# Down projection of a hybrid encoder layer as seven block products, decays from exponents of sums, the first norm scaled ahead of its transposes, and a refitted instruction order

## The chip, the cores and the metric

The kernel runs on one core of one Trainium2 chip. The metric is the time of one launch on the device in microseconds, as the median of several runs. TensorE multiplies, VectorE (DVE), ScalarE (ACT) and GpSimd (POOL) do the elementwise work, and loads and stores are issued by SyncE (SP) or by ScalarE. Products are written to PSUM, eight banks of 128 x 512 float32.

## The reference

One layer, 512 tokens, width 1024, all in float32. Cut to what matters:

```python
h = rmsnorm(x, mix_norm[l])                       # 512 x 1024
p = h @ w_in[l]                                   # 1024 x 9248
rx, ry, qkv, z, ba, gates = jnp.split(p, SPLIT_IDX, axis=-1)
y_rnn = rglru_branch(rx, ry, ...) @ w_rnn_proj[l] # conv, gates, a scan forwards and one backwards
y_dn = deltanet_branch(qkv, z, ba, ...) @ w_dn_proj[l]
x = x + (g_rnn * y_rnn + g_dn * y_dn) @ w_out[l]
h = rmsnorm(x, ffn_norm[l])
gt, up = jnp.split(h @ w_gate_up[l], 2, axis=-1)  # 2 x 2816
x = x + (jax.nn.silu(gt) * up) @ w_down[l]        # 2816 x 1024
return rmsnorm(x, final_norm)

# inside deltanet_branch, for 8 heads and both directions:
gc = jnp.cumsum(g, axis=-1)
decay = jnp.exp(jnp.where(incl, gc[..., :, None] - gc[..., None, :], -jnp.inf))
A = jnp.where(strict, jnp.einsum("nhcid,nhcjd->nhcij", kb, k) * decay, 0.0)
att = jnp.einsum("nhcid,nhcjd->nhcij", q, k) * decay
```

## The kernel before, in words

Activations lie with features on the 128 partitions and the 512 tokens along the free dimension, so a weight block of 128 x 128 is the stationary operand and 512 tokens stream. Each float32 operand is split into a high part (`whi`, `hh`, `fh`), a rounded copy that ScalarE makes, and a low part (`wlo`, `hl`, `fl`), the rest, that VectorE subtracts. A product is three matmuls: high x high, high x low and low x high. Weights come from DRAM into one of three raw tiles (`wraw`) by a load on SP's queue; the split goes into one of two pairs of tiles `whi`, `wlo`, or into tiles of the pools `t2` (14 tiles of 128 x 512) and `t4` (22 tiles of 128 x 1024). In the profile both pools read `t`.

The stages follow one another: first norm; input projection with the recurrent branch (12 blocks in groups of three) and the first heads' convolutions; four pairs of delta-net heads (`dn_front`, `dn_mats`, `dn_inverse`, `dn_state`, `dn_out`), between which the rest of the input projection and the gates run; output projection; second norm; gate and up projection; down projection; last norm.

**First norm.** `norm_scale` makes a diagonal `dg` of a token's reciprocal norm (VectorE), and `norm_transpose` multiplies the token rows by it on TensorE, which transposes and scales at once, in full float32. ScalarE then writes the high part times the gain, VectorE the low part.

**Decays.** In `dn_mats` each head and direction needs exp(gc_i - gc_j) for four chunks of 128 tokens. VectorE multiplies a triangular mask with the high and the low part of the gate column `gh`, `gl` (two 512-wide products), TensorE multiplies them with the triangular `slr` or `sur` (two 512-wide matmuls), which gives the differences of the sums, ScalarE takes the Exp of all 512 columns, and GpSimd zeroes what lies outside the triangle.

**Gate and up.** From the third k-tile of 22 on, `gate_up` already uses a seven-product form of a 2 x 2 block product (256-column matmuls): the blocks are the two halves of the contraction, gate and up, and the two halves of the tokens.

**Down projection.** For each half of the 1024 output columns `down_mm` goes through eleven pairs of k-tiles, four token chunks and three products; tokens are the stationary operand, 512 weight columns stream. The last chunk's second half is done in two pieces of 256 columns. The last three k-pairs of the second half are held so that each chunk ends by itself and its final norm (`down_end`, a root, a reciprocal, two scalings and the stores) runs while the next chunk multiplies.

**The order.** Every instruction is recorded first with a cost and a due time, and `Plan.order` then simulates the engines: the instruction with the earliest due time whose inputs are ready and whose tiles are free goes next. The due times of the stages are a table of numbers, `TIMES`; costs are formulas in `Rec.__getattr__`, times a factor `SLACK`. Where a wait between two engines is counted, `LAG` has it. Each engine then gets its instructions in that order, and so does SP's queue of loads. `spend` opens a new stage. All instructions are issued from one line of `Rec`, so the profile shows L374 throughout, and groups are told apart by their tiles.

Of the kernel before, what the change touches and what calls it, by code (L numbers as in the profile page):

```python
# [32 lines left out]
RELEASE = 200  # L33
SLACK = {"ACT": 1.1, "DVE": 1.1, "POOL": 1.2}
LOOK = 40
TIMES = [
# [18 lines left out]
class Plan:  # L55

# [5 lines left out]
    LAG = {("PE", "PE"): 0, ("PE", "DVE"): 250, ("PE", "ACT"): 250, ("DVE", "PE"): 320, ("ACT", "PE"): 320, ("POOL", "PE"): 320,  # L62
           ("DVE", "DVE"): 130, ("DVE", "ACT"): 250, ("ACT", "ACT"): 50, ("ACT", "DVE"): 200, ("DVE", "POOL"): 250,
           ("POOL", "DVE"): 150, ("ACT", "POOL"): 250, ("SP", "SP"): 0}

    def __init__(self, nc):
        self.nc = nc
        self.ops = []
        self.where, self.bases = [], []
        self.t = self.base = 0.0  # L70
# [7 lines left out]
        self.fixed = 13.3  # L78
# [40 lines left out]
    def add(self, eng, fn, outs, ins, cost, tail=0.0, table=None):  # L119
# [22 lines left out]
        cost *= SLACK.get(eng, 1.0)  # L142
        self.ops.append((eng, fn, deps, touched, round(cost), round(1.25 * tail), table, self.t))
# [3 lines left out]
    def order(self):  # L147
# [13 lines left out]
        for i, o in enumerate(ops):  # L161
            for d in o[2]:
                users[d].append(i)
        uses, first, last = {}, {}, {}
# [7 lines left out]
        need = [sorted((x for x in o[3] if x in self.tile_tag), key=first.get) for o in ops]  # L172
        free = dict(self.tags)
        queue = {tag: [] for tag in self.tags}
        for name, key in first.items():
            queue[self.tile_tag[name]].append((key, name))
# [9 lines left out]
        pe_end, cold = 0, WARM  # L186
        result, start = [], {}

        def slots(i):
            want = [x for x in need[i] if x not in held]  # L190
            taken = {}
            for name in want:
# [8 lines left out]
                for key, other in queue[tag]:  # L201
# [38 lines left out]
        while True:  # L240
            for e in ENGINES:
# [7 lines left out]
                for name in want:  # L249
# [4 lines left out]
                    queue[tag].remove((first[name], name))  # L254
                c = o[4]
                if e == "ACT" and o[6] is not None and table not in o[6]:
                    table = o[6][0]
                    c += 1283
                if e == "PE":
                    if now - pe_end > 3000:  # L260
                        cold = 0
                    if cold < WARM:
                        c *= 2
                        cold += c
                    pe_end = now + c
                end = done = now + c
# [18 lines left out]
            while events and events[0][0] == now:  # L285
                _, kind, i = heapq.heappop(events)
                o = ops[i]
                if kind == 0:
                    busy[o[0]] = False
                elif kind == 1:  # L290
# [4 lines left out]
                    for u in users[i]:  # L295
                        left[u] -= 1
                        if not left[u]:
                            wait = 0 if o[5] else self.LAG.get((o[0], ops[u][0]), 200)
# [1153 lines left out]
```

## Time and profile before

| | |
|---|---|
| median of 3 runs | 1097.39 us (1097.16 to 1097.98) |
| profiled execution, first to last instruction | 1095.2 us |
| TensorE matmuls, busy | 1070.3 us, 6916 records |
| VectorE, busy | 826.6 us, 1489 |
| ScalarE, busy | 626.6 us, 1127, of it 60 table loads 77.0 us |
| GpSimd, busy | 46.1 us, 93 |
| read from and written to DRAM | 95.17 MB and 2.10 MB |

A float32 matmul of 128 columns leaves two records, a transpose one. The stages by the trace: the first norm ends near 25 us, the recurrent groups near 250, the heads near 700, the output projection and second norm near 760, gate and up near 960, the down projection at 1089; the store of the last result ends the span. In the rows of the profile "out<-in" names the tiles without their numbers, the figure after the bar is the busy time of the group in us and the mean of one instruction in ns, and what follows is the idle time of the engine just before them with what ended it.

### The profile page before, as it was taken

What the parts mean: (1) busy time and instruction counts of PE and PEld (TensorE: products, weight loads), DVE (VectorE), ACT (ScalarE), POOL (GpSimd) and SP (SyncE); (2) the same over time, 40 slices, a digit from 0 to 9 for tenths busy, and PEclk for the clock granted to TensorE, in tenths of its full rate; (3) what the DMA queues carried; (4) which work ended last, traced back from release to release, by engine and by line L of the source; (5) the groups of instructions that cost most, each with busy time, mean ns of one, the idle gap of its engine ahead of it and who ended that gap; (6) DMA issues with size and microseconds to landing.
All of it is one profiled execution on the core that took longest, in us unless ns stands there. A gap on an engine that the chain in (4) does not pass through costs nothing.

```text
span 1095.2 us, 17616 instructions
## 1 busy us (share of the span) xinstructions
PE 1070.3 (98%) x6916; PEld 933.7 (85%) x6916; DVE 826.6 (75%) x1489; ACT 626.6 (57%) x1127; POOL 46.1 (4%) x93
## 2 busy tenths in 40 slices
PE   7999899999999999999999999999999999999997
PEld 6988678888887878788798888789999999988886
DVE  6686999669994798589759847868898988872432
ACT  6779997797346653766575254446544444451223
POOL 2000000002020010020000000000000000000000
PEclk9999999999999999999999999999999999999999
DMA  7342313232322033104211313441233334332332
GB/s 196 103 116 67 88 55 104 82 92 72 101 82 67 8 111 103 53 20 113 80 35 45 96 49 121 135 140 58 78 116 108 98 104 116 102 111 96 97 97 77
DMA packets 160787, 98.40 MB, mean 90 GB/s; under 512 B 4800, under 2 KB 151344, under 8 KB 160704
## 3 DMA queue, kind: packets, MB, share of 16 engines
q1 hardware_dynamic: 159232, 93.99, 29.6%
q10 hardware_dynamic: 1184, 3.15, 0.8%
q8 instruction: 54, 0.88, 0.3%
q14 instruction: 29, 0.24, 0.1%
q0 software_dynamic: 288, 0.13, 0.0%
HBM read 95.17 MB, written 2.10 MB: 89 GB/s over the span
## 4 chain that ended last, share of the span: by engine, by line
PE 87%; DVE 7%; ACT 4%; issue 1%; DMA 1%; SPq 0%; DVEq 0%
PE mm L374 50%; PE ax L374 22%; PE st L374 15%; DVE t L374 5%; ACT t L374 2%; DVE wlo L374 1%; ACT na L374 1%; DMA wraw<-in_w_in_dram 1%; DVE na L374 1%; ACT whi L374 1%; ACT L374 0%; DVE hl L374 0%; ACT ax L374 0%; SPq L374 0%; ACT hh L374 0%
## 5 line engine op out<-in xcount | busy, mean ns | idle before, releaser
L374 ACT CAST whi<-wraw 128x1024 fp32r<-128x1024 f32 (+2 forms) x150 | 146.6, 978 | 206.8 <-PE mm L374 83.2
L374 DVE TENSOR_TENSOR wlo<-wraw,whi 128x1024 fp32r<-128x1024 f32 (+2 forms) x149 | 168.8, 1135 | 122.3 <-ACT whi L374 75.0
L374 PE MATMUL mm<-hh,whi 128*128 128x512 f32 (+2 forms) x704 | 242.4, 356 | 3.7 <-ACT whi L374 3.6
L374 PE MATMUL mm<-hl,whi 128*128 128x512 f32 (+2 forms) x704 | 241.9, 356 | 0.0
L374 DVE TENSOR_TENSOR t<-t,t 128x512 fp32r<-128x512 f32 (+16 forms) x414 | 212.4, 524 | 17.0 <-ACT t L374 10.4
L374 PE MATMUL mm<-hh,wlo 128*128 128x512 f32 (+1 forms) x688 | 155.6, 356 | 0.0
L374 PEld LDWEIGHTS mm<-hh,whi 128*128 128x128 f32 (+1 forms) x704 | 133.0, 189 | 22.2 <-ACT whi L374 5.0
L374 PEld LDWEIGHTS mm<-hl,whi 128*128 128x128 f32 (+1 forms) x704 | 133.0, 189 | 16.9
L374 PEld LDWEIGHTS mm<-hh,wlo 128*128 128x128 f32 x688 | 115.9, 189 | 16.9
L374 DVE SCALAR_TENSOR_TENSOR t<-mm,par,t 128x511 f32<-128x511 f32 (+1 forms) x108 | 80.0, 743 | 21.0 <-ACT t L374 20.3
L374 PE MATMUL ax<-t,t 32*32 32x32 f32 (+3 forms) x876 | 90.9, 263 | 1.8 <-issue 0.8
L374 PE MATMUL mm<-t,whi 128*128 128x512 f32 x320 | 83.0, 397 | 0.6 <-DVE t L374 0.4
L374 ACT CAST t<-t 128x512 fp32r<-128x512 f32 (+1 forms) x95 | 64.7, 687 | 32.3 <-DVE t L374 29.0
L374 PEld LDWEIGHTS ax<-t,t 128*128 128x128 f32 (+1 forms) x876 | 74.2, 153 | 10.3 <-ACT t L374 2.9
L374 ACT ACT_TABLE_LOAD x60 | 77.0, 1283 | 6.4 <-PEq L1438 1.7
L374 PEld LDWEIGHTS mm<-t,whi 128*128 128x128 f32 x320 | 59.0, 188 | 14.5 <-ACT whi L374 1.9
L374 PE MATMUL mm<-t,t 128*128 128x256 f32 (+1 forms) x372 | 66.4, 322 | 0.0
L374 PEld LDWEIGHTS mm<-t,t 128*128 128x128 f32 x372 | 54.8, 191 | 4.9
L374 ACT ACTIVATE t<-t 128x128 f32<-128x128 f32 (+4 forms) x84 | 45.8, 558 | 13.0 <-DVE t L374 9.5
L374 PE MATMUL mm<-t,wlo 128*128 128x512 f32 x160 | 43.0, 393 | 0.5 <-DVE wlo L374 0.5
L374 PE MATMUL st<-hh,whi 128*128 128x512 f32 (+1 forms) x112 | 42.1, 380 | 0.3 <-ACT whi L374 0.3
L374 PE MATMUL st<-hl,whi 128*128 128x512 f32 (+1 forms) x112 | 41.7, 377 | 0.0
(219 smaller groups left out, 1808.0 us busy)
## 6 DMA issues: line engine op xcount, KB each, us to landing
wraw<-in_w_in_dram SPq DMA_DIRECT2D x72, 512.0 KB, 3.8
wraw<-in_w_gate_up_dram SPq DMA_DIRECT2D x44, 512.0 KB, 3.9
wraw<-in_w_down_dram SPq DMA_DIRECT2D x22, 512.0 KB, 3.7
wraw<-in_w_rnn_proj_dram SPq DMA_DIRECT2D x16, 384.0 KB, 3.6
wraw<-in_w_out_dram SPq DMA_DIRECT2D x8, 512.0 KB, 4.7
wraw<-in_w_dn_proj_dram SPq DMA_DIRECT2D x8, 384.0 KB, 3.5
t<-in_x_dram SPq DMA_DIRECT2D x4, 512.0 KB, 5.3
na<-in_x_dram ACTq DMA_DIRECT2D x4, 512.0 KB, 7.5
```

Source lines behind the costliest of these rows:

```text
L374: self.plan.add(e, lambda: real(*a, **kw), outs, ins, cost, tail, table)
```

## The change

Five things are changed at once.

1. The down projection is done in seven products of half-size blocks and not eight. The 2 x 2 blocks are even and odd k-tiles, the two halves of the output columns (512 each), and the two halves of the tokens (256 each). Products 1, 7, 5 and 6 go first through all eleven k-pairs, into all eight PSUM banks; then the partial sums are combined (`m_`, `v_`) into the residual, and products 2, 4 and 3 add on. `first_x` and `second_x` make the sums of activations and their splits; `down_w` loads and splits the weights of one product for two k-pairs at once.
2. The four sums of weight blocks that the products need are made earlier, by `down_sums`, while the heads run: two loads of 512 KB, four additions on VectorE, two stores of 512 KB to a scratch tensor `dsum` in DRAM for each k-pair. The down projection loads them from there.
3. The decays are no longer multiplied on TensorE. The sums of the gates, one row for each head and direction, are written to a scratch tensor `gsum` once; each head and direction loads its row broadcast to all partitions, GpSimd fills what lies outside the triangle with -1e30, and ScalarE takes four Exps of 128 columns, each with the negative sum (`ngc`) as its bias.
4. The first norm scales the token rows first (half on VectorE, half on ScalarE), and TensorE then only transposes them.
5. The planner's costs are refitted (separate occupancy and latency, longer scans and transposes, a cost for turning TensorE between tile modes, shorter waits between engines, no `SLACK`), and `TIMES` has new values, and more of them, since each step of the down projection is now a stage.

```diff
-RELEASE = 200
-SLACK = {"ACT": 1.1, "DVE": 1.1, "POOL": 1.2}
+RELEASE = 60
+TURN = 115
...
-                elif op in ("tensor_tensor", "tensor_tensor_scan"):
-                    cost = 69 + 1.042 * n
...
-                elif op == "transpose":
-                    cost = 68 + 1.042 * n
+                elif op == "tensor_tensor_scan":
+                    occ = 66 + 2.083 * n
+                elif op == "transpose":
+                    occ = 66 + (1.042 if n <= 256 else 1.99) * n
...
     def norm_scale(src, c):
-        dg = small([P, P], "dg", 4)
-        V.tensor_scalar(dg, ident, rms_rstd(src, c), None, ALU.mult)
-        return dg
+        rin = rms_rstd(src, c)
+        sc = four(shape=(P, D))
+        V.tensor_scalar(sc[:, 0:512], src[:, 0:512], rin, None, ALU.mult)
+        A.activation(sc[:, 512:D], src[:, 512:D], AF.Copy, scale=rin)
+        return sc
...
-                    T.matmul(pt[:, (2 * j + i) * P:(2 * j + i + 1) * P], srcs[i][:, kt * P:(kt + 1) * P], dgs[i], start=True, stop=True)
+                    turn(pt[:, (2 * j + i) * P:(2 * j + i + 1) * P], srcs[i][:, kt * P:(kt + 1) * P])
...
-                rh, rl = two(F32R), two(F32R)
-                mk = (upi if d == 0 else loi).unsqueeze(1).to_broadcast([P, NT, P])
-                for r_, g_ in ((rh, gh), (rl, gl)):
-                    V.tensor_tensor(r_.rearrange("p (c i) -> p c i", c=NT), mk, f(g_[:, c0:c0 + 4]).unsqueeze(2).to_broadcast([P, NT, P]), ALU.mult)
-                pd = axb()
-                lt = slr if d == 0 else sur
-                T.matmul(pd, lt, rh, start=True, stop=False)
-                T.matmul(pd, lt, rl, start=False, stop=True)
                 dt_ = two()
-                act(dt_, pd, AF.Exp)
                 dv = dt_.rearrange("p (c i) -> p c i", c=NT)
-                G.affine_select(out=dv, in_=dv, pattern=[[0, NT], [1 - 2 * d, P]], compare_op=ALU.is_ge, fill=0.0, base=0,
+                Q.dma_start(dt_, grow[d, S * h:S * (h + 1)].partition_broadcast(P))
+                G.affine_select(out=dv, in_=dv, pattern=[[0, NT], [1 - 2 * d, P]], compare_op=ALU.is_ge, fill=-1e30, base=0,
                                 channel_multiplier=2 * d - 1)
+                for c in range(NT):
+                    act(dv[:, c, :], dv[:, c, :], AF.Exp, bias=ngc[:, c0 + c:c0 + c + 1])
...
+    def down_sums(j):
+        spend()
+        now = plan.t
+        re, ro = four(shape=(P, D)), four(shape=(P, D))
...
+        Q.dma_start(re, wdn[:, 2 * j, :])
+        Q.dma_start(ro, wdn[:, 2 * j + 1, :])
...
+        V.tensor_tensor(b11, b11, b12, ALU.add)
+        V.tensor_tensor(b12, b12, b22, ALU.add)
+        V.tensor_tensor(b22, b11, b22, ALU.add)
+        V.tensor_tensor(b21, b22, b21, ALU.add)
+        Q.dma_start(dsum[j, :, 0:2, :], re.rearrange("p (a n) -> p a n", a=2))
+        Q.dma_start(dsum[j, :, 2:4, :], ro.rearrange("p (a n) -> p a n", a=2))
...
+    def first_x(j):
...
+        A.copy(xh[:, 3, :], tt[:, 0, :])
+        V.tensor_tensor(xl[:, 3, :], tt[:, 0, :], f(xh[:, 3, :]), ALU.subtract)
+        V.tensor_tensor(q[:, 0:2, :], tt[:, 0:2, :], tt[:, 1:4:2, :], ALU.subtract)
+        V.tensor_tensor(q[:, 2, :], tt[:, 0, :], q[:, 1, :], ALU.subtract)
+        V.tensor_tensor(tt[:, 1, :], tt[:, 2, :], q[:, 2, :], ALU.subtract)
+        A.copy(xh[:, 0:3, :], q[:, 0:3, :])
+        V.tensor_tensor(xl[:, 0:3, :], q[:, 0:3, :], f(xh[:, 0:3, :]), ALU.subtract)
...
+    banks = {"a": [axb(), axb()], "b": [mmb(), mmb()], "c": [stb(), stb()], "d": [axb(), mmb()]}
+    bank_of = {"1": "a", "6": "b", "7": "c", "5": "d", "2": "a", "4": "c", "3": "d"}
...
+    def down_mm(name, j, i, w, cs=(0, 1), n0=0, n=512):
+        (hi, lo), (xh, xl) = w, xp[name, j]
...
+        for c in cs:
+            po = banks[bank_of[name]][c][:, n0:n0 + n]
+            sh, sl_ = xh[:, c * P:(c + 1) * P], xl[:, c * P:(c + 1) * P]
+            T.matmul(po, sh, hi[:, i, n0:n0 + n], start=begin, stop=False, skip_group_check=sk)
+            T.matmul(po, sh, lo[:, i, n0:n0 + n], start=False, stop=False, skip_group_check=sk)
+            T.matmul(po, sl_, hi[:, i, n0:n0 + n], start=False, stop=end, skip_group_check=sk)
+
+    units = [(j, min(2, NP_ - j)) for j in range(0, NP_, 2)]
+    for j0, n in units:
+        for i in range(n):
+            first_x(j0 + i)
+        for name in ("1", "7", "5", "6"):
+            w = down_w(name, j0, n)
+            for i in range(n):
+                down_mm(name, j0 + i, i, w)
```

Three places of the order. First SP's queue where the first heads' matrices and the recurrent branch's projection are loaded (`wraw` is a weight block, `t` under `in_w_down` a raw k-tile for the sums, `gsum` and `dsum` the two scratch tensors). Before:

```order
L374 DMA wraw_396<-in_w_rnn_proj_dram 128x6x128
L374 DMA wraw_786<-in_w_in_dram 128x8x128
L374 DMA wraw_641<-in_w_in_dram 128x8x128
L374 DMA wraw_773<-in_w_in_dram 128x8x128
L374 DMA wraw_633<-in_w_in_dram 128x8x128
```

And with the change:

```order
L405 DMA t_554<-in_w_down_dram 128x1024
L405 DMA t_555<-in_w_down_dram 128x1024
L405 DMA t_689<-gsum 128x512
L405 DMA t_551<-in_w_down_dram 128x1024
L405 DMA wraw_770<-in_w_in_dram 128x8x128
L405 DMA t_550<-in_w_down_dram 128x1024
L405 DMA t_690<-gsum 128x512
L405 DMA dsum<-t_554 128x1024
L405 DMA wraw_490<-in_w_in_dram 128x8x128
L405 DMA wraw_639<-in_w_in_dram 128x8x128
L405 DMA dsum<-t_550 128x1024
```

Raw k-tiles, broadcast rows and stores of sums now stand between the weight blocks, and a store stands ahead of the next weight block's load.

Second ScalarE at the end of the recurrent branch (`rgs` marks its decay Exp, the 128x1024 forms its square roots, `st` a Gelu, `ngc` the new decays of the heads), with the change:

```order
L405 ACTIVATE t_685<-t_685,ngc_157 128x128
L405 ACT_TABLE_LOAD
L405 ACTIVATE t_494<-t_494 128x1024
L405 CAST whi_401<-wraw_400 128x768
L405 ACTIVATE t_495<-t_495 128x1024
L405 ACTIVATE t_496<-t_496 128x1024
L405 ACT_TABLE_LOAD
L405 ACTIVATE t_685<-t_685,ngc_157 128x128
L405 CAST whi_417<-wraw_416 128x768
L405 ACT_TABLE_LOAD
L405 ACTIVATE t_512<-st_513 128x512
```

Before, one Exp of 512 columns stood for the four pieces of `t_685`; now its pieces stand singly between table loads. Third TensorE in the down projection (`ax`, `st` and `mm` are PSUM banks). Before:

```order
L374 MATMUL ax_1709<-whi_1719,t_1721 128x512
L374 MATMUL ax_1709<-wlo_1720,t_1721 128x512
L374 MATMUL ax_1709<-whi_1719,t_1722 128x512
L374 MATMUL ax_1709<-whi_1719,t_1721 128x512
L374 MATMUL ax_1709<-wlo_1720,t_1721 128x512
L374 MATMUL ax_1709<-whi_1719,t_1722 128x512
```

And with the change:

```order
L405 MATMUL st_1692<-whi_1724,t_1719 128x512
L405 MATMUL ax_1688<-whi_1739,t_1733 128x512
L405 MATMUL ax_1689<-whi_1739,t_1733 128x512
L405 MATMUL st_1693<-whi_1724,t_1715 128x512
L405 MATMUL st_1693<-wlo_1725,t_1715 128x512
L405 MATMUL st_1693<-whi_1724,t_1716 128x512
L405 MATMUL st_1693<-whi_1724,t_1718 128x512
L405 MATMUL st_1693<-wlo_1725,t_1718 128x512
```

A split weight pair now serves 12 matmuls and not 24, and matmuls with the high part of the next pair (`whi_1739`) are drawn ahead of the last ones with this pair.

More of the change, by code (lines that the diff above doesn't have):

```diff
@@ L163, in order @@
                 users[d].append(i)
+        number = {name: i for i, name in enumerate(self.tile_tag)}
         uses, first, last = {}, {}, {}
@@ L200, in slots @@
                 moves, ups = [], 0
-                for key, other in queue[tag]:
+                for key, _, other in queue[tag]:
                     if other == name:
@@ L265, in order @@
                     pe_end = now + c
-                end = done = now + c
+                end, done = now + c, now + l
                 if o[5]:
@@ L289, in order @@
                     busy[o[0]] = False
+                    if o[0] == "PE":
+                        for u in users[i]:
+                            if ops[u][0] == "PE":
+                                left[u] -= 1
+                                if not left[u]:
+                                    insort(ready["PE"], (when[u], u))
                 elif kind == 1:
@@ L516, in trunk @@
     for c0 in (0, 2):
-        norm_transpose(xs[c0:c0 + 2], [norm_scale(xs[c0 + i], i) for i in range(2)], gain, hh, hl, c0)
-        plan.t = -15.0
-    plan.t = 0.0
+        xs = []
+        for c in (c0, c0 + 1):
+            xc = four(shape=(P, D))
+            Q.dma_start(xc, x[0, c * P:(c + 1) * P, :])
+            xs.append(xc)
+        if c0 == 0:
+            gain = load_gain(mix_norm[0], "gain1")
+        norm_transpose([norm_scale(xs[i], i) for i in range(2)], gain, hh, hl, c0)
+        spend()
     prow = two(shape=(P, 2, P))
@@ L1109, in trunk @@
     for g in range(4):
+        for j in range(3 * g, min(3 * g + 3, NP_)):
+            down_sums(j)
         spend()
@@ new lines, in raw_part, with down_w @@
+    def raw_part(par, half):
+        return lambda j, n: wdn[:, 2 * j + par:2 * j + par + 2 * n - 1:2, 512 * half:512 * (half + 1)]
+    wsrc = {"1": raw_part(0, 0), "2": raw_part(1, 0), "3": raw_part(1, 1), "4": sum_part(2), "5": sum_part(0), "6": sum_part(3), "7": sum_part(1)}
+    def down_w(name, j, n, held=False):
+        now = plan.t
+        raw = new(wp, (P, 2, 512), "wraw", 3)
+        if held:
+            hi, lo = four(F32R), four(F32R)
+        else:
+            hi, lo = new(wp, (P, 2, 512), "whi", 2, F32R), new(wp, (P, 2, 512), "wlo", 2, F32R)
+        plan.t = now - 40
+        Q.dma_start(raw[:, 0:n, :], wsrc[name](j, n))
+        plan.t = now - AHEAD
+        A.copy(hi[:, 0:n, :], raw[:, 0:n, :])
+        V.tensor_tensor(lo[:, 0:n, :], raw[:, 0:n, :], f(hi[:, 0:n, :]), ALU.subtract)
+        plan.t = now
+        return hi, lo
@@ new lines, in second_x @@
+    def second_x(j):
+        now = plan.t
+        plan.t = now - AHEAD
+        tt = fa[j].rearrange("p a (h t) -> p (a h) t", h=2)
+        xh = four(F32R, (P, 4, 256))
+        xl = four(F32R, (P, 4, 256)) if j < 3 else keep[(j - 3) // 4][:, 2 * ((j - 3) % 4):, :][:, 0:2, :].rearrange("p a (h t) -> p (a h) t", h=2)
+        plan.admit = (xh, xl)
+        A.copy(xh[:, 0:3, :], tt[:, 1:4, :])
+        plan.admit = ()
+        V.tensor_tensor(xl[:, 0:3, :], tt[:, 1:4, :], f(xh[:, 0:3, :]), ALU.subtract)
+        plan.t = now
+        for i, name in enumerate("324"):
+            xp[name, j] = xh[:, i, :], xl[:, i, :]
@@ L1412, in trunk @@
-        act(rst, ssf[:, c, 2 if c == NT - 1 else 1:][:, 0:1], AF.Sqrt, scale=1.0 / D, bias=rst)
+        for k in range(1, parts - 1):
+            V.scalar_tensor_tensor(rst, ssf[:, c, k:k + 1], 1.0 / D, rst, ALU.mult, ALU.add)
+        act(rst, ssf[:, c, parts - 1:parts], AF.Sqrt, scale=1.0 / D, bias=rst)
         V.reciprocal(rin, rst)
```

260 lines of the change are left out of this document (162 added, 98 removed), and 27 rows, old and new, of the table TIMES.

## The prediction

> **What bounds the kernel now.** I read the spans and clocks first, then the page's busy times and chain of waits, then the busy time of each engine by stage, then TensorE's own waits.
>
> ```profile
> core 0: 1095.2 us, clock 0.997
> ```
> ```profile
> PE 1070.3 (98%) x6916; PEld 933.7 (85%) x6916; DVE 826.6 (75%) x1489; ACT 626.6 (57%) x1127; POOL 46.1 (4%) x93
> ...
> PE 87%; DVE 7%; ACT 4%; issue 1%; DMA 1%; SPq 0%; DVEq 0%
> ```
> ```profile
> core 0: us, PE busy (x) PEld busy (x) DVE busy (x) ACT busy (x) POOL busy (x), PEclk, DMA share, GB/s
> 0.00:25.00 25.00, 17.67 (x113) 15.99 (x114) 15.35 (x40) 16.90 (x36) 6.65 (x21) 1.00 0.76 202
> ...
> 100.00:125.00 25.00, 21.36 (x86) 16.87 (x85) 21.44 (x24) 20.96 (x28) 0.00 (x0) 0.93 0.19 53
> 125.00:250.00 125.00, 124.54 (x554) 101.27 (x553) 104.97 (x120) 105.74 (x162) 2.07 (x4) 1.00 0.31 89
> 250.00:700.00 450.00, 442.75 (x3070) 370.06 (x3069) 355.21 (x777) 245.46 (x520) 36.78 (x66) 1.00 0.26 73
> ...
> 760.00:958.00 198.00, 198.00 (x1652) 198.00 (x1652) 176.11 (x308) 97.32 (x176) 0.00 (x0) 1.00 0.35 102
> 958.00:1089.00 131.00, 130.95 (x679) 112.53 (x678) 53.69 (x70) 43.17 (x58) 0.00 (x0) 1.00 0.29 95
> 1089.00:1095.20 6.20, 0.00 (x0) 0.00 (x0) 1.46 (x4) 1.52 (x4) 0.00 (x0) 0.66 0.32 113
> ```
> TensorE is the bound in every stage. Its idle time is 7.3 us in the first 25 us, 6.2 us after its last matmul, and 11.4 us between: 3.64 + 0.46 + 7.25 + 0.05 from the rows 100:125, 125:250, 250:700 and 958:1089. The granted clock is 1.00 except in 100:125, where 0.93 of 25 us is 1.7 us lost. So TensorE work taken out of a dense stage comes off the end one for one, while the other engines hold still. Who holds TensorE up:
>
> ```profile
> PE ax L374 <- DVE dg L374: 3.9, 2, 3.6
> PE mm L374 <- ACT whi L374: 3.6, 2, 2.5
> PE ax L374 <- DVE t L374: 3.6, 5, 0.9
> ```
>
> **The change, part by part.**
>
> *Down projection.* Chain pieces at the pace of the two widths:
>
> ```profile
> 952.35 4.32 PE mm L374 x36
> ...
> 992.72 2.72 PE st L374 x12
> ```
> A 512-column matmul takes 2.72/12 = 0.227 us, a 256-column one 4.32/36 = 0.120 us. The instruction order has 462 wide and 132 narrow matmuls for this projection before, 453 and 18 after. That removes 9 x 0.227 + 114 x 0.120 = 15.7 us from a stage with 130.95 of 131 us busy. **Term: -15.7.** The other bound is 0, if the feed of the matmuls becomes the limit. The feed by these rows (VectorE's subtractions of one low half, its smaller operations, ScalarE's cast; then the loads, now and in two busier stretches):
>
> ```profile
> L374 DVE TENSOR_TENSOR wlo<-wraw,whi 128x1024 fp32r<-128x1024 f32 x18 | 22.0, 1224 | 56.3 <-ACT whi L374 56.3
> ```
> ```profile
> L374 DVE TENSOR_TENSOR t<-t,t 128x512 f32<-128x512 f32 x56 | 38.3, 685 | 1.5 <-ACT t L374 1.3
> ...
> L374 DVE TENSOR_TENSOR wlo<-wraw,whi 128x768 fp32r<-128x768 f32 x24 | 22.9, 954 | 21.6 <-ACT t L374 11.5 <-ACT whi L374 6.7 <-PE mm L374 1.7
> ...
> L374 DVE TENSOR_TENSOR t<-ax,t 128x256 f32<-128x256 f32 x40 | 16.8, 422 | 13.5 <-PE ax L374 13.4
> ...
> L374 ACT CAST t<-wraw 128x1024 fp32r<-128x1024 f32 x9 | 9.5, 1059 | 5.9 <-DMA wraw<-in_w_out_dram 3.7 <-DMA wraw<-in_w_gate_up_dram 1.6 <-DMA wraw<-in_w_down_dram 0.7
> ```
> ```profile
> wraw<-in_w_down_dram SPq DMA_DIRECT2D x22, 512.0 KB, 3.7
> ```
> ```profile
> 700.00:725.00 25.00, 25.00 (x112) 20.72 (x111) 17.37 (x26) 10.89 (x16) 0.00 (x0) 1.00 0.64 191
> ```
> ```profile
> wraw<-in_w_gate_up_dram SPq DMA_DIRECT2D x6, 512.0 KB, 5.0
> ```
> In the first half (products 1, 7, 5, 6) two k-pairs are 48 matmuls, 10.9 us. VectorE owes them four low halves (4 x 1.224) and twice the activation sums and splits (0.685 + 3 x 0.422 + 0.954): 10.7 us, 98% of the time. These means count the overlap of neighbours twice; the gate/up stage runs TensorE 198 of 198 us with VectorE busy 176.11, so I take it that 98% by means still fits. In the second half it is 3 x 1.224 + 2 x 0.954 = 5.6 of 8.2 us. The weights come as 35 loads of 512 KB and 7 of 256 KB, 20.2 MB in 104.9 us: 192 GB/s where it was 95. At 191 GB/s, in 700:725, TensorE stayed full. The three raw buffers allow a load L, a cast and a subtraction every 3 x 2.72 = 8.2 us, so L may be 8.2 - 1.06 - 1.22 = 5.9 us; measured medians are 3.7 here and 5.0 in the stretch 690:735. It is covered, by 0.9 us at the worse value. The Trainium skill's page "DMA: Bandwidth & Descriptors", section "Latency and other measured facts", states 0.2 us HBM latency on average and 2 us at high load. By it the 3.7 would become an estimated 5.5 us, and 0.4 us of cover would remain; the two medians agree with the direction.
>
> *Weight sums.* Eleven k-pairs, each two 512 KB loads, four 512-wide VectorE additions, two 512 KB stores. VectorE: 44 x 0.685 = 30.1 us, placed between 250 and 700, behind TensorE's 442.75 us while VectorE has 355.21 of 450 busy. *Decays.* Gone are 32 wide matmuls (32 x 0.227 = 7.3 us) and 32 VectorE products; come 16 broadcast loads and 64 128-wide Exps for 16 wide ones:
>
> ```profile
> L374 DVE TENSOR_TENSOR t<-upi,gh 128x512 fp32r<-128x512 f32 x8 | 5.9, 741 | 0.0
> ...
> L374 DVE TENSOR_TENSOR t<-loi,gl 128x512 fp32r<-128x512 f32 x8 | 5.5, 687 | 3.5 <-ACT t L374 3.5
> ```
> ```profile
> L374 ACT ACT_TABLE_LOAD x60 | 77.0, 1283 | 6.4 <-PEq L1438 1.7 <-PE ax L374 1.5 <-DVE so L374 1.3
> ...
> L374 ACT ACTIVATE t<-t,rgs 128x512 f32<-128x512 f32 x24 | 16.0, 716 | 0.1
> ...
> L374 ACT ACTIVATE t<-ax 128x512 f32<-128x512 f32 x20 | 12.0, 598 | 8.4 <-PE ax L374 8.2
> ...
> L374 ACT ACTIVATE t<-t 128x128 f32<-128x128 f32 x32 | 9.6, 302 | 7.8 <-DVE t L374 6.3 <-PE ax L374 1.5
> ```
> VectorE loses about 32 x 0.71 = 22.7 us, so with the sums it gains 7 us in 450 and stays at 81%. ScalarE gets 64 x 0.30 - 16 x 0.60 = 9.7 us, or 15.8 us if the bias pointer costs the 0.1 us by which 716 exceeds the row of 598 ns; and 14 more table loads, 14 x 1.283 = 18.0 us. By the instruction order three of the loads come before the first square root of a head's norms (at 252 us in the trace) and eleven behind it, where ScalarE is busy 245.46 of 450 us, so nearly all of it lies beside TensorE. **Term: -7.3**, the other bound 0; what the loads cost without cover is the third rival. The mask on GpSimd now comes ahead of the Exp and waits for a broadcast load instead of a matmul and an Exp:
>
> ```profile
> L374 POOL TENSOR_SCALAR_AFFINE_SELECT t<-t 128x512 f32<-128x512 f32 x16 | 15.9, 999 | 144.4 <-ACT t L374 134.7 <-DVE t L374 9.7
> ```
> Behind it on GpSimd stand the scalings of keys that the state's matmuls wait for. GpSimd is busy 36.78 of 450 us and the load needs only the sums of the start, so I cost that wait at nothing; uncovered it would be one load, 3.7 us by the 512 KB row, at each of the four head pairs.
>
> *First norm.*
>
> ```profile
> L374 PE MATMUL ax<-ident,t 128*128 128x128 f32 x162 | 24.2, 273 | 0.8 <-ACT ax L374 0.8
> ...
> L374 PE MATMUL ax<-dg,t 128*128 128x128 f32 x64 | 11.2, 335 | 4.4 <-DVE dg L374 3.9 <-DVE rin L374 0.4 <-DVE hl L374 0.2
> ```
> ```profile
> 15.45 1.34 PE ax L374 x12
> ```
> The 32 products by a diagonal leave 64 records of 1.34/12 = 0.112 us, so 0.224 us each; a transpose leaves one record. That saves 32 x 0.112 = 3.6 us, half of it while TensorE waits anyway (7.3 us idle in 0:25). **Term: -1.8.** Bounds: -7.3 if the idle time went with it, since the first full weight block is now asked for third on SP's queue and not sixth; +2.9 if ScalarE's four half-row scalings (4 x 0.716) delay the evictions.
>
> *Refitted order.* The planner's costs change most where it was wrong:
>
> ```profile
> L374 DVE TENSOR_TENSOR_SCAN t<-t,t 128x512 f32<-128x512 f32 x24 | 28.4, 1212 | 0.0
> ...
> L374 DVE STREAM_TRANSPOSE t<-t 128x1024 f32<-128x1024 f32 x12 | 25.3, 2152 | 0.1
> ```
> It had 663 ns for the scan and 1249 ns for this transpose (by its formula with its factor 1.1), and has now 1133 and 2104. The wait for `whi` (3.6 us) and the lost clock (1.7 us) stand in 100:125, beside scans. I take these 5.3 us as gone, and half of that, 2.7 us, as given back in the down projection's first half, where VectorE has no room. **Term: -2.6.** Bounds: -13.1 (11.4 + 1.7, all stalls), and +18.0 if each of the 14 table loads fell on TensorE's path.
>
> Sum: -15.7 - 7.3 - 1.8 - 2.6 = -27.4; the span becomes 1067.8. The median before lies 2.2 us above the profiled span (1097.39 and 1095.2), so **1070.0 us**.
>
> **The rivals.**
>
> *The down projection stays feed-bound.* For it: VectorE's 98%, twice the traffic, two pairs of split buffers where a pair now lasts 2.72 us and not 5.4. Against it: the dense 191 GB/s stretch. Decisive point: loads over 5.9 us, or any operation in front of a subtraction by over a microsecond. If the whole gain goes, 1070.0 + 15.7 = 1085.7.
>
> *All stalls go.* The new costs are near the trace's durations, and many more due times are set by hand for the down projection. 1070.0 - 13.1 + 2.6 = 1059.5. Against it: new stalls come with each new dependence.
>
> *The order does not do what it is fitted to do.* The three table loads ahead of 252 us fall where ScalarE is busy 105.74 of 125 us: 3 x 1.283 = 3.9 us. If they push the casts that TensorE waits for, and the 5.3 us of stalls stay, 1070.0 + 5.3 + 3.9 = 1079.2. For it: single Exps of 128 columns stand between two table loads. Against it: eleven of fourteen lie where ScalarE has room. A load is followed by work at once in the chain of waits:
>
> ```profile
> 101.01 1.28 ACT L374
> 102.29 0.01 issue
> 102.31 1.07 ACT t L374
> ```
> The skill's page "ScalarE: Activation LUTs", section "What ACT_TABLE_LOAD costs", states about 1283 ns and a drain of 1380 ns for each switch. The first agrees; no drain shows behind this load, and with one the estimate of this case would be 3 x 1.38 = 4.1 us later.
>
> *Slower: stores on SP's queue.* The 22 stores of sums wait there for VectorE, and every weight load behind them waits too. Time goes to TensorE only when the delay exceeds what is staged ahead, some 24 matmuls or 5.4 us for one weight block. To pass 1099.6 it has to eat 29.6 us, 1.35 us for each store with none hidden. For it: 2.7 us of additions stand before each pair of stores. Against it: three raw buffers, and VectorE at 81%.
>
> **How the numbers follow.** Forecast 0.64, feed-bound 0.15, all stalls gone 0.10, order no better 0.07, slower 0.04. The range 1060 to 1084 holds the forecast with its start term anywhere between its bounds (1064.5 to 1074.7), the order case, the feed-bound case up to nine tenths of its loss, and half of the all-stalls case; what is left out is the other half, the full feed-bound loss and the slower case, below 0.2. Within 0.2% (2.2 us, about what a measurement of this kernel can tell from no change) I put 0.03, where two of the bad cases meet; faster 0.93, slower 0.04.
>
> **What would show it.** Down stage near 105 us with TensorE full; its idle there is the feed-bound case, and then `wlo` or the raw loads end the waits. Between 250 and 700 about 7 us less TensorE work, and no wait of `whi` for a raw load behind a store. No clock under 1.00 after the start. I am wrong if TensorE's idle time inside the span exceeds some 20 us, or if the matmuls keep another pace than 0.227 us.

## The result and the profile after

The changed kernel takes 1072.6 us (median of 4 runs, 1072.36 to 1072.80) against 1097.68 us before on the same chip: ratio 0.977, 95% interval 0.9759 to 0.9782. The forecast was 1070.0 us in a range of 1060 to 1084. Beside later experiments the changed kernel took 1072.56 us again. Its spans and clocks:

```profile
core 0: 1070.4 us, clock 0.998
```

The span is 24.8 us shorter, where the sum of the prediction was 27.4. The page's busy times and its chain of waits:

```profile
PE 1047.6 (98%) x6730; PEld 906.4 (85%) x6730; DVE 884.3 (83%) x1584; ACT 684.5 (64%) x1238; POOL 49.7 (5%) x93
...
PE 71%; DVE 15%; ACT 9%; issue 3%; DMA 1%; ACTq 0%; DVEq 0%
```

TensorE still has 98%, but the chain that ended last now runs through VectorE and ScalarE for 24% of the span; it was 11%. Where TensorE waits, the windows tell (each row: the window in us, its length, then the busy time of TensorE, its weight loads, VectorE, ScalarE and GpSimd, with the number of instructions in brackets, then the granted clock, the DMA share and GB/s):

```profile
0.00:25.00 25.00, 16.68 (x107) 15.46 (x108) 15.64 (x37) 18.40 (x37) 6.84 (x21) 1.00 0.78 211
100.00:125.00 25.00, 24.99 (x109) 20.00 (x108) 24.97 (x31) 24.77 (x31) 0.00 (x0) 1.00 0.29 80
125.00:250.00 125.00, 124.28 (x556) 101.41 (x555) 106.22 (x126) 115.59 (x193) 14.83 (x11) 1.00 0.43 127
250.00:700.00 450.00, 445.34 (x3074) 371.73 (x3073) 367.17 (x795) 263.07 (x552) 27.43 (x60) 1.00 0.42 129
700.00:952.00 252.00, 252.00 (x2002) 247.05 (x2002) 218.97 (x382) 126.60 (x233) 0.00 (x0) 1.00 0.34 100
952.00:1002.00 50.00, 50.00 (x226) 40.68 (x225) 43.73 (x67) 28.85 (x37) 0.00 (x0) 1.00 0.52 167
1002.00:1027.00 25.00, 23.65 (x99) 17.54 (x98) 22.14 (x29) 17.93 (x25) 0.00 (x0) 1.00 0.62 190
1027.00:1063.50 36.50, 35.80 (x163) 28.60 (x161) 26.67 (x38) 19.16 (x31) 0.00 (x0) 1.00 0.54 173
1063.50:1070.40 6.90, 0.00 (x0) 0.00 (x0) 2.56 (x10) 2.54 (x8) 0.00 (x0) 0.69 0.43 152
```

The stall and the lost clock of 100:125 are gone (24.99 of 25 us, clock 1.00). The new down projection starts at 951.9 us; for its first 50 us TensorE is full, and then it stands still for 1.35 us in 1002:1027 and 0.70 us in 1027:1063.5.

Busy time hides a part of the loss, because a matmul that starts late still counts as busy by its neighbours' ends. So the following table is worked out from the starts of successive matmuls in the two traces: the time from one start to the next, less 0.227 us for 512 columns, 0.120 for 256, 0.11 for 128 and 0.01 to 0.03 for smaller ones, summed by stage. It is the time that TensorE lost against a dense stream.

| stage | lost before | lost after |
|---|---|---|
| 0 to 25 us | 8.7 | 10.1 |
| 25 to 100 | 1.2 | 2.4 |
| 100 to 125 | 5.8 | 0.6 |
| 125 to 250 | 2.1 | 2.1 |
| 250 to 700 | 24.9 | 23.3 |
| 700 to the down projection | 0.0 | 0.6 |
| down projection | 0.1 | 5.1 |
| matmul work at full pace, all stages | 1043.0 | 1016.6 |

The work at full pace fell by 26.4 us: 15.7 in the down projection, 7.3 for the decays and 3.5 in the first norm, as the instruction order had said. Lost time rose by 1.3 us, the end after the last matmul grew from 6.2 to 6.9 us, and the first matmul came 0.3 us earlier. The one large entry that rose is the down projection: from its first wide matmul to the end of the last 111.6 us (with 12 narrow ones of gate and up, 1.4 us, among them), where the prediction had 104.9; before, 123.8 us (with 24 such, 2.9 us). Without these 120.9 became 110.1, so 10.8 of the 15.7 us were kept.

### The profile page after: what moved, and what is told of

It reads as the page before. It is cut to its first block, busy times and chain, and to the rows that moved or that the text cites. A ratio compares the mean times of both kernels' runs of the same rounds, so it can differ in the third digit from the quotient of the medians.

```text
span 1070.4 us, 17691 instructions
## 1 busy us (share of the span) xinstructions
PE 1047.6 (98%) x6730; PEld 906.4 (85%) x6730; DVE 884.3 (83%) x1584; ACT 684.5 (64%) x1238; POOL 49.7 (5%) x93
## 4 chain that ended last, share of the span: by engine, by line
PE 71%; DVE 15%; ACT 9%; issue 3%; DMA 1%; ACTq 0%; DVEq 0%
PE mm L405 36%; PE ax L405 22%; PE st L405 14%; DVE t L405 11%; ACT t L405 4%; DVE wlo L405 3%; ACT na L405 1%; ACT L405 1%; ACT whi L405 1%; DVE na L405 0%; DMA wraw<-in_w_out_dram 0%; DMA t<-in_x_dram 0%; DVE hh L405 0%; ACTq L405 0%; ACT hh L405 0%
## 5 line engine op out<-in xcount | busy, mean ns | idle before, releaser
L405 DVE TENSOR_TENSOR t<-t,t 128x512 fp32r<-128x512 f32 (+19 forms) x480 | 245.6, 530 | 28.9 <-ACT t L405 23.8
L405 ACT CAST whi<-wraw 128x1024 fp32r<-128x1024 f32 (+3 forms) x171 | 165.8, 970 | 157.0 <-PE mm L405 72.6
L405 DVE TENSOR_TENSOR wlo<-wraw,whi 128x1024 fp32r<-128x1024 f32 (+3 forms) x170 | 191.3, 1126 | 45.5 <-ACT whi L405 34.9
L405 ACT CAST t<-t 128x512 fp32r<-128x512 f32 (+3 forms) x117 | 75.5, 655 | 49.7 <-DVE t L405 42.6
L405 PE MATMUL mm<-t,whi 128*128 128x512 f32 x320 | 85.9, 397 | 0.8 <-DVE t L405 0.6
L405 ACT ACTIVATE t<-t 128x128 f32<-128x128 f32 (+4 forms) x84 | 45.5, 556 | 26.5 <-DVE t L405 23.7
L405 PE MATMUL mm<-t,t 128*128 128x256 f32 (+1 forms) x348 | 59.0, 315 | 0.2 <-DVE t L405 0.2
L405 PEld LDWEIGHTS mm<-t,t 128*128 128x128 f32 x348 | 49.7, 191 | 5.0 <-DVE t L405 0.9
L405 PE MATMUL ax<-whi,t 128*128 128x512 f32 x137 | 47.3, 395 | 1.2 <-ACT whi L405 1.2
```

The source lines that it names most:

```text
L405: self.plan.add(e, lambda: real(*a, **kw), outs, ins, occ, lat, tail, table, mode)
```

## The experiments

**Undoing one part at a time.** The edits of the three runs that undo a part are given in words. In the first the old down projection returns:

```diff
-    down_sums for each k-pair; products 1, 7, 5, 6 and 2, 4, 3, weights from w_down and dsum
+    down_mm over two halves of the columns, eleven k-pairs, four chunks
```

> The changed kernel with the old down projection: 462 wide and 132 narrow matmuls again, no weight sums, no loads and stores of them. Theory (TensorE's sum sets the time, and the new down projection kept 10.8 of its 15.7 us because about 5 us went to waits in it): 1072.6 + 10.8 = 1083.4 us, with TensorE full in the old projection. Rival (the 30 us of VectorE additions and 22 MB of loads and 11.5 MB of stores between 250 and 700 us cost time of their own there): less than that, 1075 to 1081 us, because they go too. Rival (the 5 us were not lost in the projection but moved there by the order): 1072.6 + 15.7 = 1088.3 us.

Measured: 1083.31 us (1082.2 to 1083.75), ratio 0.9872 (0.9858 to 0.9887): 10.7 us more than the changed kernel, as the first theory had it. A window of this kernel, the same stretch as above:

```profile
1002.00:1027.00 25.00, 25.00 (x123) 21.14 (x123) 9.89 (x16) 7.95 (x13) 0.00 (x0) 1.00 0.32 106
```

TensorE is full there with VectorE at 9.89 of 25 us instead of 22.14. The weight sums between 250 and 700 us show no cost of their own: they are gone too, and by the starts of the matmuls TensorE lost 23.7 us in that stretch without them and 23.3 with them. The other stages up to 700 us keep their loss within 0.1 us, so this edit left the order there as it was.

In the next one the old first norm returns:

```diff
-    rows scaled by rin (VectorE and ScalarE), then 32 transposes
+    dg = ident * rin (VectorE), then 32 products by dg
```

> The changed kernel with the old first norm: rows transposed by products with a diagonal (64 records of TensorE for 32 of them), no scaling of rows ahead. Theory (the whole of the 3.6 us of matmul work does not count, because TensorE waits in the first 15 us anyway; the start stage was 2.1 us shorter after the change): 1072.6 + 2.1 = 1074.7 us. Rival (the scaling ahead of the transposes costs what it saves): 1072.6 us. Rival (work for work): 1076.2 us.

Measured: 1073.8 us (1072.21 to 1074.59), ratio 0.9785 (0.9771 to 0.98). The 1.2 us lie between the first two cases, and the intervals of the two kernels overlap. The starts of the matmuls say how: 3.5 us more work, and 7.7 instead of 10.1 us lost in the first 25 us.

Undoing the decays (the two masked factors lie in one tile of `t4` and the differences in an `mm` bank; with the tiles that the kernel before used for them, two of `t2` and an `ax` bank, the planner found no order):

```diff
-    broadcast load of a gsum row; fill with -1e30 outside the triangle; 4 Exps of 128 with a bias
+    mask * gh and mask * gl; 2 matmuls; Exp of 512; fill with 0 outside the triangle
```

> The changed kernel with the old decays: 32 wide matmuls again (their accumulators in the banks of the projections, their two factors in one buffer of the pool of four), 32 masked products on VectorE, 16 wide exponentials on ScalarE instead of 64 narrow ones and 16 broadcast loads. Theory (TensorE's sum sets the time): 1072.6 + 7.3 = 1079.9 us. Rival (the 14 extra table loads of the new form were partly on TensorE's path): less, 1072.6 + 7.3 - 3.9 = 1076.0 us. Rival (VectorE's 22.7 us come back and it is full beside the weight sums): more than 1082 us, with TensorE idle between 250 and 700 us.

Measured: 1115.99 us (1115.05 to 1118.21), 43 us above the changed kernel and far above the first two cases. By its time it would fit the third, more than 1082 us. Two windows of this kernel:

```profile
350.00:400.00 50.00, 39.51 (x171) 31.11 (x171) 39.82 (x83) 34.30 (x78) 8.54 (x16) 0.86 0.37 122
...
550.00:600.00 50.00, 39.23 (x422) 32.95 (x421) 20.77 (x50) 28.14 (x77) 4.19 (x12) 0.86 0.16 43
```

TensorE stands still for 10.5 and 10.8 us there and loses clock (0.86) on top. VectorE is not full in them (39.82 and 20.77 of 50), so the reason that the third case gave is not there. My reading is that the due times were set for the instructions of the changed kernel, and that with other tiles in the heads' stage the order fell apart. That is argued, not shown, and the run says nothing on the price of the decays.

So that price was taken without touching the order. Each instruction keeps its place on every engine, and two wide matmuls are issued ahead of every second score product, 32 in all, into a bank that the score product then overwrites (`fn` issues it, `po` is its bank):

```diff
+            for i in range(2):
+                nc.tensor.matmul(po, hh[:, 0, 0:P], hh[:, 0, :], start=True, stop=True)
+            fn()
...
+                    if c2 == 0:
+                        twice(pk)
```

> The changed kernel with exactly its order on every engine, and 32 wide matmuls more: two ahead of each pair of score matmuls between 250 and 700 us, into a bank that the score matmuls then overwrite, as many as the old decays had. 32 x 0.227 = 7.3 us. Theory (TensorE's work there comes off or on the end one for one): 1072.6 + 7.3 = 1079.9 us. Rival (TensorE's lost 23.3 us of that stretch are waits on the other engines, which would absorb part of it): 1073 to 1077 us.

Measured: 1079.54 us (1079.11 to 1080.91), ratio 0.9836 (0.9819 to 0.9853): 7.0 us over the changed kernel for 7.3 us of work. Although TensorE loses some 23 us in that stretch to small matmuls and waits, next to nothing of the added work was absorbed. On VectorE, ScalarE and GpSimd the trace has the same instructions in the same order as in the changed kernel.

**Which part of the refitted order?** The kernel before, with the new constants and cost formulas of the planner alone, and `TIMES` as it was:

```diff
-RELEASE = 200
-SLACK = {"ACT": 1.1, "DVE": 1.1, "POOL": 1.2}
+RELEASE = 60
+TURN = 115
...
```

> The kernel before with the planner's new costs and constants alone, its due times untouched and its work unchanged. Theory (the stall and the half clock at 100 to 125 us came from the planner's wrong durations of the scan and the wide transpose): 5.3 us off, 1097.7 - 5.3 = 1092.4 us, and no clock under 1.00 in 100:125. Rival (they went because the due times were set anew): no change, 1097.7 us, or slower, because the old due times were made for the old costs.

Measured: 1100.58 us (1099.95 to 1101.37), ratio 1.003 (1.0017 to 1.0043), slower. Three windows of it:

```profile
100.00:125.00 25.00, 22.99 (x101) 18.37 (x100) 24.20 (x28) 20.26 (x28) 0.00 (x0) 1.00 0.21 56
...
700.00:760.00 60.00, 58.73 (x333) 50.85 (x332) 46.57 (x74) 35.43 (x64) 0.00 (x0) 1.00 0.41 123
760.00:971.00 211.00, 209.72 (x1738) 209.14 (x1737) 184.85 (x318) 102.57 (x184) 0.00 (x0) 1.00 0.35 101
```

The clock in 100:125 is whole and the loss there falls from 5.8 to 2.6 us, so the costs had a share in the stall. But TensorE now waits where it had been full (1.27 us in 700:760, 1.28 in 760:971), and by the starts of the matmuls the loss of all stages rose by 4.4 us, 3.1 of them between 250 and 700 us. The costs alone are worth nothing here. Whether new due times would have paid without them was not run.

**Why the down projection kept only two thirds.** The waits of TensorE's weight loads in this stage of the changed kernel, in us in total, times, longest:

```profile
PEld ax L405 <- ACT whi L405: 3.5, 8, 1.1
PEld ax L405 <- DVE wlo L405: 1.1, 2, 1.0
PEld st L405 <- DVE wlo L405: 1.0, 3, 0.6
```

They name the split of the weights. It is not the loads behind it: one cast of this stage waited for a load, 0.8 us, and the medians from issue to landing are as forecast:

```profile
wraw<-dsum SPq DMA_DIRECT2D x20, 512.0 KB, 3.8
wraw<-in_w_down_dram SPq DMA_DIRECT2D x15, 512.0 KB, 3.7
```

TensorE's rows at one such place:

```profile
1015.84 0.39 PE L405 MATMUL mm<-whi,t 128*128 128x512 f32 x1
1016.54 0.50 PE L405 MATMUL ax<-whi,t 128*128 128x512 f32 x1 [0.31 <-ACT whi L405]
1016.88 0.40 PE L405 MATMUL mm<-whi,t 128*128 128x512 f32 x1
1017.49 0.50 PE L405 MATMUL ax<-whi,t 128*128 128x512 f32 x1 [0.21 <-ACT whi L405]
```

Starts 0.70 and 0.61 us apart instead of 0.227. Three things meet between 1002 and 1027 us: the last units of the first four products, which hold one k-pair and not two; twelve 512-wide sums on VectorE that carry the eight finished banks over; and the splits of the activations for the second half. The first two were tried apart. The third was not, though three of its casts, 2.3 us, stand on ScalarE right ahead of the cast that ended the wait at 1016.54. For the sums, half of them went to an idle engine:

```diff
-        V.tensor_tensor(xv, xv, m_[:, c, :], ALU.add)      # and five like it
+        G.tensor_tensor(xv, xv, m_[:, c, :], ALU.add)
```

> Between the two halves of the new down projection VectorE has twelve 512-wide sums; six of them take both factors from SBUF and go to GpSimd, which is idle there. TensorE lost 3.0 us at 1002 to 1027 us of the changed kernel's profile. Theory (these sums on top of a VectorE that is already full by its durations): 1.5 to 3 us off, 1069.6 to 1071.1 us, and less excess of TensorE in that stretch. Rival (the half-filled split buffers of the eleventh k-pair): no change, 1072.6 us, and the same waits for the split weights at 1012 to 1018 us. Rival (the loads): no change either, and a wait for a raw load before the cast.

Measured: 1076.03 us (1075.83 to 1076.24), ratio 0.9804 (0.9789 to 0.9819), 3.4 us slower, against every case. VectorE's groups while GpSimd adds (1016.7 to 1027.4 us), GpSimd's row, and TensorE's main wait from 1002 to 1064 us, in this kernel:

```profile
L405 DVE TENSOR_TENSOR wlo<-wraw,whi 128x1024 fp32r<-128x1024 f32 x3 | 6.4, 2127 | 0.0
L405 DVE TENSOR_TENSOR wlo<-wraw,whi 128x512 fp32r<-128x512 f32 x1 | 1.5, 1455 | 0.0
...
L405 DVE TENSOR_TENSOR t<-t,st 128x512 f32<-128x512 f32 x2 | 1.3, 674 | 0.0
```
```profile
1016.70 10.67 POOL L405 TENSOR_TENSOR na<-na,t 128x512 f32<-128x512 f32 x6 [467.03 <-DVE t L405]
```
```profile
PE ax L405 <- DVE wlo L405: 3.0, 4, 1.2
```

And in the changed kernel, in the same windows:

```profile
L405 DVE TENSOR_TENSOR wlo<-wraw,whi 128x1024 fp32r<-128x1024 f32 x4 | 4.9, 1222 | 0.0
...
L405 DVE TENSOR_TENSOR t<-t,st 128x512 f32<-128x512 f32 x2 | 1.4, 680 | 0.0
L405 DVE TENSOR_TENSOR wlo<-wraw,whi 128x512 fp32r<-128x512 f32 x1 | 0.7, 682 | 0.0
```
```profile
PE ax L405 <- DVE wlo L405: 0.5, 1, 0.5
```

While GpSimd adds (1.78 us each on average), a 512-wide subtraction of VectorE with both inputs in SBUF takes 1.46 us (0.68 in the changed kernel), a 1024-wide one 2.13 on average (1.22). The two operations that read a bank (`st`) keep their 0.67 us. The Trainium skill's page "SBUF — State Buffer", section "SBUF: two separate sides", says that VectorE operations with two SBUF inputs and GpSimd operations that read SBUF share a port pair under an exclusive lock, and that the later one is blocked for the whole instruction; the trace agrees, down to the operations that read PSUM and are spared: the 512-wide subtraction starts 0.38 us into the first addition and ends 0.55 us after it. So the six sums took 4.1 us off VectorE, and the stretching put about 4 us back on the subtractions that TensorE waits for: its loss in 1002:1027 doubled from 3.0 to 6.0 us. Whether the twelve sums cause a part of the changed kernel's loss stays open by this test; that the time of VectorE's subtractions there is on the path, it shows.

For the single units, their split buffers come from the larger pool:

```diff
-        if held:
+        if held or n == 1:
             hi, lo = four(F32R), four(F32R)
```

> The eleventh k-pair of the down projection stands alone: its seven units have 6 matmuls (1.36 us) for one split pair of buffers where the others have 12 (2.72 us). Here these units take their two split buffers from the pool of four instead of the two pairs whi and wlo. Theory of the buffers: the waits at 1012 to 1018 us and at 1046 to 1052 us go, 1.5 to 2.5 us off, 1070.1 to 1071.1 us. Rival (VectorE's twelve sums between the halves): the stretch at 1046 to 1052 us at most, 1.1 us, and 1012 to 1018 us as before. Rival (the pool of four is full there, and the units wait for a free buffer): slower than 1072.6 us.

Measured: 1072.54 us (1071.67 to 1073.41), ratio 0.9772 (0.9758 to 0.9787): no change. Yet the waits moved. The only wait of TensorE's matmuls that is left behind 1027 us in this kernel:

```profile
1059.00 0.38 PE L405 MATMUL mm<-t,t 128*128 128x256 f32 x1 [1.08 <-DVE t L405]
```

By the starts of the matmuls the loss in 1002:1027 fell from 3.0 to 2.1 us, the 1.1 us at 1046 to 1052 us vanished, and 1.2 us came back at the last unit, whose split stands on VectorE behind the row ends of two chunks: its raw tile comes free too late to be ordered ahead of them. So in the next run that tile went to the larger pool too:

```diff
-        raw = new(wp, (P, 2, 512), "wraw", 3)
+        raw = four() if held else new(wp, (P, 2, 512), "wraw", 3)
```

> As the run with the eleventh pair's split buffers in the pool of four, which took away the waits at 1012 to 1018 us and 1046 to 1052 us and got a new one of 1.24 us at 1058 us for it; now the last two units' raw buffers lie in that pool too, so that their split is ordered ahead of the row ends of the third and fourth row block. Theory (the wait at 1058 us is the split that stands behind these row ends on VectorE and ScalarE): 1.2 us less there, and 1.5 to 3 us below the changed kernel, 1069.6 to 1071.1 us. Rival (VectorE's and ScalarE's work in the stage is what counts, and each wait taken away comes back elsewhere): 1072 to 1073 us.

Measured: 1071.92 us (1071.12 to 1072.62), ratio 0.9764 (0.9748 to 0.9781): 0.7 us under the changed kernel, but the runs and the intervals of the two overlap, so the time alone does not tell them apart. The windows of this kernel:

```profile
1002.00:1027.00 25.00, 24.11 (x102) 18.25 (x101) 20.91 (x27) 17.24 (x23) 0.00 (x0) 1.00 0.73 230
1027.00:1061.60 34.60, 34.56 (x159) 28.04 (x157) 27.52 (x40) 20.34 (x34) 0.00 (x0) 1.00 0.48 153
1061.60:1069.40 7.80, 0.00 (x0) 0.00 (x0) 3.35 (x10) 2.66 (x7) 0.00 (x0) 0.65 0.38 134
```

The last matmul ends 1.9 us earlier than in the changed kernel and the loss of the stage falls from 5.1 to 3.5 us, but the end after it grows from 6.9 to 7.8 us, because the row ends that stood in front now stand behind. By the traces both theories have a part: the buffers of the single units held about 1.6 us of TensorE's time, and half of that came back as the end. What is left of the loss, some 3.5 us, is 0.9 us of waits for VectorE's split at 1006 and 1018 us and many starts late by less than 0.17 us each; their cause was not tried apart.

**The start.** In the changed kernel the matmuls behind 9 us keep half pace although the profile shows a clock of 1.00 there; starts 0.21 us apart for 256 columns, until the pace jumps at 15 us:

```profile
14.16 0.41 PE L405 MATMUL mm<-hl,whi 128*128 128x256 f32 x1
14.37 0.41 PE L405 MATMUL mm<-hh,whi 128*128 128x256 f32 x1
...
14.96 0.29 PE L405 MATMUL mm<-hl,whi 128*128 128x256 f32 x1
15.08 0.28 PE L405 MATMUL mm<-hh,whi 128*128 128x256 f32 x1
```

Could TensorE be made ready earlier?

```diff
+    wb = axb()
+    for i in range(32):
+        T.transpose(wb[:, 0:P], ident, ident)
```

> 32 transposes of the identity into an unused bank, as soon as the identity is made (2.6 us), so that TensorE does not stand still until the first rows come at 6.9 us. In the changed kernel the matmuls between 9.1 and 14.8 us keep half pace (0.21 us for each 256-column one, 0.12 from 15.0 us) after TensorE had stood still for most of the first 9 us. Theory (half pace is the state after standing still, and it ends some 3.4 to 6 us after work begins): the matmuls at 11 to 15 us go at 0.12, and 1 to 2.8 us come off, 1069.8 to 1071.6 us. Rival (the pace there is set by what the matmuls wait for): no change in the pace and none in the time, 1072.6 us. Rival (the extra work delays the first transposes): slower by up to 1.5 us.

Measured: 1075.7 us (1075.37 to 1076.51), ratio 0.98 (0.9784 to 0.9816), the third case and twice its price. Windows of this kernel, 23 transposes in 4.9 us and then ten records in 0.9 us:

```profile
2.60:7.50 4.90, 4.90 (x23) 4.90 (x24) 0.00 (x0) 2.07 (x5) 4.11 (x9) 1.00 1.05 347
7.70:8.60 0.90, 0.90 (x10) 0.79 (x8) 0.00 (x0) 0.00 (x0) 0.33 (x1) 1.00 1.10 346
11.90:13.70 1.80, 1.77 (x9) 1.77 (x10) 1.23 (x1) 1.65 (x5) 0.00 (x0) 0.50 1.07 213
```

The pace doubles 5.0 us after the first transpose, but the transpose of the gain stood behind all 32, VectorE's copy of the gain waited 6.4 us for it, and the rows behind that copy came 2.9 us late; with waits of 0.85 and 1.63 us on TensorE, half pace was back at 11.9 us (now recorded: 0.50). The same with 28 transposes behind that of the gain:

> 28 transposes of the identity again, now behind the transpose of the gain and no longer ahead of it: in the earlier run VectorE's copy of the gain, and behind it the scaling of the rows, stood 2.9 us late. There TensorE went at half pace (0.213 us for each transpose) for 5.0 us and then at 0.109. Theory (half pace ends some 5 us after work begins, and comes back when TensorE stands still for about 2 us): the transposes run from 2.8 to 8.3 us, the first rows' matmuls at 11 to 15 us keep 0.12 us, and 1 to 2.3 us come off, 1070.3 to 1071.6 us. Rival (the wait of 1.3 us behind the first three rows' transposes is enough to bring half pace back): 1072.6 us. Rival (what the matmuls at 11 to 15 us wait for is late by itself): full pace with gaps, 1072.6 us.

Measured: 1071.3 us (1070.81 to 1071.55), ratio 0.976 (0.9744 to 0.9776). TensorE's rows of this kernel:

```profile
3.00 5.53 PE L405 MATMUL ax<-ident 128*128 128x128 f32 x28
8.37 2.05 PE L405 MATMUL ax<-ident,t 128*128 128x128 f32 x12
...
12.54 0.28 PE L405 MATMUL mm<-hl,whi 128*128 128x256 f32 x1
12.66 0.29 PE L405 MATMUL mm<-hh,whi 128*128 128x256 f32 x1
```

Full pace from 7.6 us on, 0.12 us between the starts at 12.5 us; it is held through the start, and 1.3 us come off, as the theory had it, though the intervals of the ratios overlap. More did not come off because TensorE now waits 1.3 us for VectorE's `hl` (0.3 in the changed kernel), which the slow pace had hidden.

**Both helps together**, the last two edits, beside the changed kernel on the same chip:

> The 28 transposes of the identity at the start and the eleventh pair's buffers (split and last raw ones) in the pool of four, together. Theory (the two lie 900 us apart and TensorE sets the time throughout): their gains of 1.2 to 1.3 us (first wide matmul of the down projection at 950.7 instead of 951.9 us) and 1.0 us (profiled span 1069.4 instead of 1070.4 us) add, 1072.6 - 2.3 = 1070.3 us. Rival (the row ends after the last matmul, which came 0.9 us later in the one, take more): 1071.3 us.

Measured: 1070.77 us (1070.61 to 1070.91), ratio 0.976 (0.9746 to 0.9773); the changed kernel beside it 1072.56 us (1072.33 to 1073.75), ratio 0.9778 (0.9765 to 0.9792). The runs do not overlap, the intervals of the ratios do: 1.8 us or 0.17%, between the two cases and at the edge of what can be told.

## Why the prediction came out as it did

**Right in its frame.** TensorE's work sets the end. The two runs that change this work and leave the order of the rest much as it was bear it out: 10.7 us for the down projection, 7.0 for 32 matmuls of 7.3 us. The sum missed by 2.6 us, and 1072.6 lies within the likeliest case. Of the miss 2.2 us are the down projection: -13.0 with the 2.7 us given back there, -10.8 measured. That the rest came out within 0.4 us is in part luck. Shifts that the sum did not have cancel in it: by the table -1.6 us in 250:700, +1.2 in 25:100 and +0.6 ahead of the down projection, and +0.7 at the end.

**The signs named ahead.** The granted clock is 1.00 in every window of the trace up to the last matmul, and the pace stayed at 0.227 us. TensorE stands idle for 7.6 us between 25 us and its last matmul; with the start (8.3) and the end (6.9) it is 22.8, over the limit of some 20 us if these are counted, but the kernel before had 24.9 by that count.

**The down projection, -15.7: the term that was mis-sized.** The work went as counted; 5.1 us were lost, net -10.8. The step that failed is the cover by averages. By the windows VectorE has 43.73 of 50 us in the first half proper, so the 98% by means was 87%, and only 0.5 us was lost there. But 3.0 us were lost in 1002:1027 and 1.5 behind it. The averages left out the seam: the eleventh k-pair alone, whose unit lasts 1.36 us and not 2.72 in two pairs of buffers (1.6 us of loss, by the runs that gave it more). They left out the twelve sums and the splits for the second half beside them as well; what share of the loss is theirs is not shown.

**The 2.7 us "given back in the down projection's first half"** were the right idea with half the size, and mostly at the seam instead. The feed-bound rival with its full 15.7 us did not come: its decisive point, loads over 5.9 us, was not reached (3.7 and 3.8 us), and TensorE stayed full for 50 us at 167 GB/s. Its other point, an operation of over a microsecond in front of a split, came at the seam in kind: the three casts of 2.3 us together.

**Decays, -7.3.** The price of the matmuls is confirmed by the added ones, not by undoing the decays. The two costs on ScalarE, by form:

```profile
L405 ACT ACT_TABLE_LOAD x74 | 94.9, 1283 | 7.1 <-DVE so L405 2.4 <-PE mm L405 1.9 <-PEq L1604 1.7
...
L405 ACT ACTIVATE t<-t,ngc 128x128 f32<-128x128 f32 x64 | 21.5, 393 | 1.5 <-POOL t L405 1.4
```

Fourteen more table loads, 18 us, and Exps of 393 ns, the upper of the two estimates; TensorE's loss in 250:700 nevertheless fell from 24.9 to 23.3 us. So no cost of the wait on GpSimd and of the loads shows in that stage. That they cost nothing by themselves is not shown: the order was refitted at the same time, and the one run without them fell apart.

**First norm, -1.8.** Between -1.2 (undone, where the intervals overlap) and -2.1 (work less the loss of the start). Right in size, though the reason was half known: the prediction took the granted clock of 1.00 in the first 25 us as full pace, and the time there hangs on half pace and on VectorE.

**Refitted order, -2.6.** The 5.3 us of 100:125 went as said (5.8 to 0.6 lost). The reason given, that the planner had been wrong on the scan and the transpose, explains only a part: with these costs alone that loss fell to 2.6 us and the old kernel as a whole became slower. Of the loss elsewhere, outside the down projection, 1.6 us went and 3.2 came (1.4 in the first 25 us, 1.2 in 25:100, 0.6 ahead of the down projection).

**Slower by stores on SP's queue.** It did not come. Two casts of ScalarE between 250 and 700 us waited for a raw load, first in the changed kernel, then in the run with the old down projection, which has no store of a sum:

```profile
ACT whi L405 <- DMA wraw<-in_w_in_dram: 6.6, 2, 3.5
```
```profile
ACT whi L405 <- DMA wraw<-in_w_in_dram: 6.8, 2, 3.4
```

The two waits stand at the same places, at 312 and 316 us, without a store, so they are not what the rival describes, and the sign "no wait of `whi` for a raw load behind a store" holds.

## What to carry to other kernels

Cover by averages holds in the middle of a long loop and fails at its seams: cost the first and last unit, the odd one and the hand-over between two phases by themselves, with the buffers that they hold. An order fitted to one program is part of that program: one undone piece left the rest as it was, another cost 43 us. Compare the lost time stage by stage before such a difference is read as a price, or add work to the same order. Before work is moved to an idle engine, look at whether both engines read the same memory at that moment.

## What the runs showed of the hardware that was not expected

GpSimd's SBUF additions stretched VectorE's two-input SBUF subtractions from 0.68 to 1.46 us (512 wide) and from 1.22 to 2.13 us (1024 wide), and its operations with an input in PSUM not at all (0.68 and 0.67 us).

In the two runs with transposes at the start, TensorE begins at half pace and doubles it 5.0 us (first transpose at 2.56 us) and 4.6 us (at 3.0 us) after it starts to work; transposes count as work. Two waits of 0.85 and 1.63 us, with three transposes between them, brought half pace back. The Trainium skill's page "TensorE: Matmul & The Clock Gate", section "What's actually happening", states about 3.4 us of sustained work for the one and at least one idle window of about 3.4 us for the other; both differ here, the first by 1.2 to 1.6 us, and for the second the longest wait between full and half pace was 1.63 us. And the granted clock in the windows reads 1.00 through this first half pace: starts 0.213 us apart tell it, that column does not.
